# A hybrid decoder layer on one core: the last three planned blocks are ordered with lagging engines and loads, and the output stage's last operand is made behind its second product

## The chip, the cores and the metric

The kernel runs on one core of one Trainium2 chip. The core has five engines with a queue each: TensorE (PE, matrix products; its weight loads are listed as PEld), VectorE (DVE), ScalarE (ACT), GpSimd (POOL) and SyncE (SP), which here issues the DMAs. Every engine works through its own queue in order, and an instruction waits on semaphores for what other engines or DMAs must have finished. The metric is the device time of one execution, in microseconds (us), taken as the median of several runs. Before the change it is 1078.72 us.

## What is computed

One layer over 1024 rows of width 1024, all in 32-bit floats. The input is normalised and modulated, projected, and goes through four mixers A to D; each mixer's output, gated, is projected back to the full width by its `w_br`, weighted by a sigmoid gate from `h @ w_merge`, and summed. One last projection, a gate per column and a final norm follow:

```python
mod = (jax.nn.silu(c) @ w_ada + b_ada)[:, None, :]
shift, scale, gate = jnp.split(mod, 3, axis=-1)
h = rms_norm(x, norm_g) * (1.0 + scale) + shift
...                     # h @ w_in, split into 16 parts, four mixers
merged = None
for i, (y, z) in enumerate(branches):
    yi = y.reshape(B, S, BRANCH_W) * jax.nn.silu(z)
    term = jax.nn.sigmoid(h @ w_merge[i]) * (yi @ w_br[i])
    merged = term if merged is None else merged + term
x = x + gate * (merged @ w_out)
return rms_norm(x, final_g)
```

Four products of 1024 x 1024 x 1024 with `w_merge` and one with `w_out` are the bulk of the second half of the kernel, which is the half that the change touches.

## The kernel before, in words

**Products.** A 32-bit operand is split into a rounded high part and a low part: ScalarE copies the source into the high tile (`whi<-wst`), and VectorE or GpSimd subtracts to get the low tile (`wlo<-wst,whi`). A product is then three passes of matmuls, high x high, high x low and low x high. The 2 x 2 block products are done in seven products in place of eight: sums and differences of blocks are formed first (`s<-wst`, `wst<-wst,wst`), and sums of results after. One `product` (12 matmuls of 128 x 512: four depths of three passes) fills one bank of TensorE's output memory; the banks are called `s`, `t`, `d`, `y` with a number, and VectorE adds a finished bank to a tile `mt`, which frees it. `op(n)` makes the split of the stationary operand of product n, with the sums that it needs.

**Stages.** The first block holds everything up to the mixers and ends near 583 us. The *pair stage* (`noted(tc, 8000.0)` at L1824, 582 to 938 us) takes 14 pairs of output tiles, seven products each, 98 in all. `op(7 * q + 6)` ends a pair's operands and calls for the merge weights of a later pair: two loads of 512 KB, into the tiles `wst` 0 and 1, which are the only two, so that a load waits for the split that reads the last content. Small loads `pst` (128 KB, `w_br`) and `ga` (`w_ada`) go out between them on the same queue. The modulation's gate is summed up here too, on VectorE (`gate_sum`), and finished column by column with a 128 x 1 matmul (`gate_end`); behind the eighth the vector `gatec` is written to DRAM as `gd`, 1024 elements of four bytes.

The *merge tail* (`noted(tc)` at L1884, 938 to 985 us) does the two output tiles left over without the seven-product form, loads `w_out` (`wr`, four loads of 1 MB) and prepares its sums and splits (`tt`, `hh`, `hl`, `yh`, `yl`). The *output stage* (`noted(tc)` at L1957, 985 to 1078 us) makes four groups of seven products with `w_out`, numbers 102 to 129. Its last moving operand is `wt4`, split from the parts that the tail left in `wst`; then `gd` and `final_g` are loaded over them, spread on all partitions (`gateb`, `fgb`), and VectorE multiplies the results by `gateb`, adds `x`, and writes the normed rows out.

**What sets the order.** Each block is first only noted: `note` records every instruction with its label, its predecessors and an estimated length. `schedule` then plays the block through with these estimates: an engine takes, of its ready instructions, the one with the lowest priority number, and the resulting starts set the order of emission. A priority is the rank of noting plus a number from a table, `SHIFT_PE` for TensorE and `SHIFT` for the others, looked up by the label, such as `('op', 97)`, `('out', 106)` (a product and what follows it), or `('tile', 3)`; a label that isn't in the table gets 0 or 10000. `late` is the time to which VectorE, ScalarE and GpSimd are taken to be busy with the block before; TensorE and SyncE are taken as free at 0. Every instruction is emitted by one line of `issue`, L380 before, L426 in the changed kernel, so that the profile tells groups apart by their tiles alone.

Of the kernel before, what the change touches and what calls it, by code (L numbers as in the profile page):

```python
# [88 lines left out]
def chunks(w):  # L89
# [28 lines left out]
    ('item', 3): 3000, ('item', 4): 1000, ('item', 7): 100, ('item', 9): 7000, ('out', 102): -10000,  # L118
    ('out', 103): 330, ('out', 106): -10030, ('out', 107): 10000, ('out', 109): 0, ('out', 110): 0,
    ('out', 111): 3000, ('out', 112): 9987, ('out', 113): 30, ('out', 114): 10000,  # L120
    ('out', 115): 10000, ('out', 117): -10, ('out', 119): -10890, ('out', 120): -30,
    ('out', 121): 3000, ('out', 122): -10000, ('out', 123): 10027, ('out', 124): 294,
    ('out', 126): -10800, ('out', 128): 10000, ('out', 129): 10000, ('out', 94): 0,
    ('out', 95): -10, ('out', 96): 10303, ('out', 97): -13, ('sum', 1): 9900, ('sum', 2): -10000,
    ('tile', 0): -9700, ('tile', 1): 3936, ('tile', 10): -10030, ('tile', 11): -9727,
    ('tile', 13): 10000, ('tile', 14): 0, ('tile', 15): -370, ('tile', 16): -10000,
    ('tile', 17): 9700, ('tile', 18): -10400, ('tile', 19): 0, ('tile', 21): -100,
    ('tile', 25): 10600, ('tile', 26): 9970, ('tile', 27): -400, ('tile', 28): 0,
# [26 lines left out]
    ('item', 28): -10010, ('item', 29): 20000, ('item', 3): 3000, ('item', 30): 10100,  # L155
# [4 lines left out]
    ('mod', 6): -10, ('mod', 7): 20000, ('mod', 8): 0, ('op', 100): -1000, ('op', 101): 100,  # L160
# [5 lines left out]
    ('op', 98): -9980, ('op', 99): 10, ('out', 102): 10100, ('out', 103): -1000, ('out', 104): 30,  # L166
    ('out', 107): -9863, ('out', 108): 10, ('out', 109): 0, ('out', 110): 10000, ('out', 111): 0,
    ('out', 112): -300, ('out', 113): 0, ('out', 114): -3, ('out', 115): 10000, ('out', 116): 2700,
    ('out', 118): 10, ('out', 119): 30, ('out', 120): 10970, ('out', 121): -10030,
    ('out', 122): 3000, ('out', 123): 0, ('out', 124): 30, ('out', 126): -10, ('out', 129): 9990,  # L170
    ('out', 93): 0, ('out', 94): -10100, ('out', 95): 30, ('out', 96): -103, ('out', 97): 8990,
    ('split', 0): 0, ('split', 1): 30, ('split', 2): 9700, ('split', 3): 1000, ('split', 4): -10300,
    ('split', 5): 0, ('split', 6): -100, ('sum', 0): 0, ('sum', 1): 0, ('sums', 0): 9700,
    ('sums', 1): 10097, ('sums', 2): 2057, ('tile', 15): 19630, ('tile', 23): -1300,
# [260 lines left out]
def hybrid_kernel(ctx: ExitStack, tc: tile.TileContext, x, c, w_ada, b_ada, norm_g, w_in, cmp_pos,  # L435
                  cmp_w1, cmp_w2, sink, w_merge, w_br, w_out, final_g, kb, km, kd, ks, kw, out):
    nc = tc.nc
    md = Program()
# [564 lines left out]
    with ac:  # L1003
# [607 lines left out]
    with ExitStack() as mc:  # L1611
# [449 lines left out]
```

## Time and profile before

| what | before |
|---|---|
| median of 3 runs | 1078.72 us (1078.55 to 1079.52) |
| profiled execution | 1079.71 us, its span 1077.9 us |
| TensorE busy | 1040.4 us, 97% of the span |
| VectorE, ScalarE, GpSimd busy | 796.5, 584.4 and 435.5 us |
| mean granted clock of TensorE | 0.988 |
| moved by DMA | 105.47 MB |

The span runs from the first to the last instruction; the profiled execution's time has 1.8 us more around it. Busy TensorE time counts matmuls, which are pipelined: a matmul of 128 x 512 lasts 0.39 us in the records, but the next starts about 0.23 us behind it when the clock is at its full 2.4 GHz, and 0.43 us behind it at 1.2 GHz, the lower of the two levels. The granted clock of a stretch is 1.00 when it was at the upper level throughout.

### The profile page before, as it was taken

The numbers are of one execution on the slowest core, as the hardware profiler recorded it, in microseconds if no ns is written. First come the engines' busy times: TensorE is split into PE (matmuls) and PEld (weight loads), VectorE is DVE, ScalarE is ACT, GpSimd is POOL, SyncE is SP. The second block draws the span as 40 slices with busy tenths as digits, with TensorE's granted clock in tenths as the row PEclk, the third lists the DMA queues.
The fourth block names the chain that finished last, engine by engine and source line by source line (L and its number), as shares of the span: only waits on it lengthen the run. The fifth ranks groups of instructions, "written<-read, shape, count | busy, mean of one in ns | idle before, by whom it ended". The sixth has DMA issues, their size and how long they took to land.

```text
span 1077.9 us, 16022 instructions
## 1 busy us (share of the span) xinstructions
PE 1040.4 (97%) x5391; PEld 873.4 (81%) x5391; DVE 796.5 (74%) x1797; ACT 584.4 (54%) x1281; POOL 435.5 (40%) x483
## 2 busy tenths in 40 slices
PE   5999999999999999999999999999999999998996
PEld 4778888889878898888888788888888888876885
DVE  5559976986558877999875346777785565489897
ACT  5699964994348866767874232333333233346343
POOL 4623214213525466655464122255454555430002
PEclk8999999999999999999999999999999999999998
DMA  9763311102321113314313913322322232262232
GB/s 338 259 201 80 83 25 48 33 21 59 54 79 40 30 40 101 107 62 134 103 55 124 350 53 88 98 69 69 88 88 58 54 90 73 73 230 74 77 107 95
DMA packets 117606, 105.47 MB, mean 98 GB/s; under 512 B 15260, under 2 KB 96212, under 8 KB 116756
## 3 DMA queue, kind: packets, MB, share of 16 engines
q1 hardware_dynamic: 116048, 99.95, 30.3%
q0 software_dynamic: 1408, 4.48, 1.3%
q8 instruction: 42, 0.69, 0.3%
q14 instruction: 40, 0.33, 0.1%
q10 hardware_dynamic: 68, 0.02, 0.0%
HBM read 81.88 MB, written 17.83 MB: 93 GB/s over the span
## 4 chain that ended last, share of the span: by engine, by line
PE 70%; DVE 11%; ACT 6%; issue 5%; DMA 5%; POOL 2%; SPq 1%; POOLq 0%; ACTq 0%; DVEq 0%
PE d L380 25%; PE s L380 22%; PE t L380 14%; PE y L380 8%; DVE SP L380 4%; ACT t L380 2%; DVE lo L380 1%; DMA wst<-in_w_merge_dram 1%; DVE t L380 1%; ACT SP L380 1%; ACT whi L380 1%; DVE FA L380 1%; POOL RA L380 1%; DMA RA<-RA 1%; ACT hi L380 1%
## 5 line engine op out<-in xcount | busy, mean ns | idle before, releaser
L380 POOL TENSOR_TENSOR wlo<-wst,whi 128x512 fp32r<-128x512 f32 (+1 forms) x108 | 143.3, 1337 | 214.4 <-ACT whi L380 208.8
L380 PE MATMUL d<-hh,whi 128*128 128x512 f32 x440 | 180.5, 410 | 2.5 <-ACT hh L380 1.8
L380 ACT ACTIVATE whi<-wst 128x512 fp32r<-128x512 f32 (+2 forms) x121 | 89.0, 739 | 164.7 <-PE s L380 47.3
L380 PE MATMUL d<-hh,wlo 128*128 128x512 f32 x440 | 173.4, 394 | 0.0
L380 PE MATMUL d<-hl,whi 128*128 128x512 f32 x440 | 173.0, 394 | 0.0
L380 PEld LDWEIGHTS d<-hh,wlo 128*128 128x128 f32 x440 | 83.4, 190 | 18.7
L380 PEld LDWEIGHTS d<-hh,whi 128*128 128x128 f32 x440 | 83.6, 190 | 15.3 <-ACT hh L380 2.0
L380 DVE TENSOR_TENSOR lo<-t,hi 128x512 fp32r<-128x512 f32 (+2 forms) x132 | 79.8, 624 | 18.2 <-ACT hi L380 17.4
L380 PEld LDWEIGHTS d<-hl,whi 128*128 128x128 f32 x440 | 83.5, 190 | 11.6 <-DVE hl L380 0.4
L380 ACT ACTIVATE hi<-t 128x512 fp32r<-128x512 f32 (+3 forms) x148 | 73.8, 525 | 31.4 <-PE t L380 26.9
L380 POOL TENSOR_TENSOR acc<-acc,mt 128x512 f32<-128x512 f32 x44 | 68.0, 1547 | 44.3 <-DVE mt L380 43.7
L380 PE MATMUL s<-hh,whi 128*128 128x512 f32 x200 | 80.4, 402 | 3.9 <-ACT whi L380 3.9
L380 PE MATMUL s<-hh,wlo 128*128 128x512 f32 x200 | 79.7, 398 | 0.9 <-DVE wlo L380 0.9
L380 PE MATMUL s<-hl,whi 128*128 128x512 f32 x200 | 78.5, 394 | 0.0
L380 PE MATMUL t<-kbt,SP 128*128 128x128 f32 (+1 forms) x470 | 68.3, 274 | 6.8 <-DMA kbt<-in_kb_dram 6.4
L380 POOL TENSOR_SCALAR SP<-SP,den,gates 128x640 f32<-128x640 f32 (+7 forms) x64 | 52.9, 835 | 52.9 <-DVE den L380 20.7
L380 ACT ACTIVATE SP<-SP,mx 128x257 f32<-128x257 f32 (+9 forms) x96 | 62.3, 651 | 11.9 <-DVE mx L380 10.7
L380 DVE TENSOR_TENSOR mt<-s,mt 128x512 f32<-128x512 f32 x61 | 41.2, 686 | 36.4 <-PE s L380 36.1
L380 PEld LDWEIGHTS t<-kbt,SP 128*128 128x128 f32 (+1 forms) x470 | 54.7, 141 | 14.2 <-DMA kbt<-in_kb_dram 6.4
L380 PE MATMUL s<-tt,whi 128*128 128x512 f32 x192 | 59.1, 389 | 0.0
L380 ACT ACTIVATE mt<-mt 128x512 f32<-128x512 f32 x56 | 35.1, 629 | 35.4 <-DVE mt L380 35.2
L380 ACT ACTIVATE t<-t 128x512 f32<-128x512 f32 (+5 forms) x97 | 50.1, 522 | 1.1
(343 smaller groups left out, 2717.7 us busy)
## 6 DMA issues: line engine op xcount, KB each, us to landing
wst<-in_w_merge_dram SPq DMA_DIRECT2D x32, 512.0 KB, 4.8
wst<-in_w_in_dram SPq DMA_DIRECT2D x26, 512.0 KB, 3.9
td<-FA SPq DMA_DIRECT2D x32, 256.0 KB, 2.4
tt<-td SPq DMA_DIRECT2D x6, 1024.0 KB, 10.2
FA<-in_x_dram SPq DMA_DIRECT2D x8, 512.0 KB, 5.5
pst<-in_w_br_dram SPq DMA_DIRECT2D x32, 128.0 KB, 2.2
ga<-in_w_ada_dram SPq DMA_DIRECT2D x16, 256.0 KB, 3.1
wr<-in_w_out_dram SPq DMA_DIRECT2D x4, 1024.0 KB, 9.1
```

The lines of the kernel that those rows point to most:

```text
L380: fn(*args, **kw)
```

## The change

Both tables get new entries for the pair stage, the tail and the output stage (some 80 and some 170 labels that had none); those of the first block stay, and so does the first block's order. `schedule` takes TensorE's clock as full from the start and the first DMA as busy until `late + 1100` wherever `late` is set; the tail gets `late` 2000 and the output stage 6000, where both had 0. In `pair`, `op(7 * q + 6)` is noted ahead of the fourth product and of the `yield`; for the last pair, whose rest is noted in the tail, this moves that call into the pair stage. In the output stage the `wt4` parts and the loads of `gateb` and `fgb` are noted behind the second product instead of at the start.

```diff
@@ SHIFT_PE, SHIFT
-    ('tile', 4): 20000, ('tile', 5): 10300, ('tile', 6): -10000, ('tile', 7): 1000,
+    ('tile', 8): 0, ('tile', 9): -2700,
...
@@ schedule
-        dma = warm = 0.0
+        dma, warm = (self.late + 1100.0, 3400.0) if self.late else (0.0, 0.0)
@@ pair
             add(u3, o, u2)
+            op(7 * q + 6)
             yield
             o = product(7 * q + 3, MOVING[3])
-            op(7 * q + 6)
             add(g11, o, t1)
@@ merge tail
-        with md.noted(tc):
+        with md.noted(tc, 2000.0):
             for t, kh, n in ((r11, 0, 0), (r12, 0, 1), (r22, 1, 1), (r21, 1, 0)):
@@ output stage
-        with md.noted(tc):
-            md.label = "wt4", 0
-            for k in range(4):
-                parts(wt4, k, t4f[k], ve)
-            sy.dma_start(gateb, gd.partition_broadcast(P))
-            sy.dma_start(fgb, final_g.partition_broadcast(P))
+        with md.noted(tc, 6000.0):
             x_load(0)
...
                 o = product(b + 1, MOVING[1])
                 op(b + 4)
+                if q == 0:
+                    md.label = "wt4", 0
+                    for k in range(4):
+                        parts(wt4, k, t4f[k], ve)
+                    sy.dma_start(gateb, gd.partition_broadcast(P))
+                    sy.dma_start(fgb, final_g.partition_broadcast(P))
                 add(u2, o, t1)
```

The number of instructions is the same on every engine; what follows is their order at three places.

SyncE's queue in the pair stage, around the write of `gd` (`wst_125` and `wst_126` are the two tiles for merge weights). Before:

```order
L380 DMA wst_125<-in_w_merge_dram 128x8x128
L380 DMA wst_126<-in_w_merge_dram 128x8x128
L380 DMA gd<-gatec 128x8x1
L380 DMA pst_5774<-in_w_br_dram 128x2x128
L380 DMA pst_5776<-in_w_br_dram 128x2x128
L380 DMA wst_125<-in_w_merge_dram 128x8x128
L380 DMA wst_126<-in_w_merge_dram 128x8x128
```

And in the changed kernel:

```order
L426 DMA wst_125<-in_w_merge_dram 128x8x128
L426 DMA gd<-gatec 128x8x1
L426 DMA wst_126<-in_w_merge_dram 128x8x128
L426 DMA pst_5774<-in_w_br_dram 128x2x128
L426 DMA pst_5776<-in_w_br_dram 128x2x128
L426 DMA pst_5774<-in_w_br_dram 128x2x128
L426 DMA wst_125<-in_w_merge_dram 128x8x128
L426 DMA wst_126<-in_w_merge_dram 128x8x128
```

Before, `gd` is followed by two `pst` loads and then by the two merge loads of a later pair; now the first of these two stands ahead of `gd` and the second directly behind it.

VectorE at the same place, from the gate sum on (`s_5801<-wst_126` reads the merge load just spoken of; `d_132` and `d_133` are two of TensorE's banks). Before:

```order
L380 TENSOR_TENSOR gatec<-d_133,gatec 128x1
L380 SCALAR_TENSOR_TENSOR mt_5806<-mt_5806,y_137 128x512
L380 TENSOR_TENSOR mt_5803<-s_136,mt_5802 128x512
L380 TENSOR_TENSOR wlo_142<-wst_125,whi_141 128x512
L380 TENSOR_TENSOR mt_5807<-t_127,mt_5803 128x512
L380 TENSOR_TENSOR mt_5805<-t_140,mt_5802 128x512
L380 TENSOR_TENSOR mt_5802<-d_132,mt_5803 128x512
L380 TENSOR_TENSOR mt_5804<-d_132,mt_5807 128x512
L380 TENSOR_TENSOR s_5801<-wst_126 128x512
L380 SCALAR_TENSOR_TENSOR mt_5805<-mt_5805,d_133 128x512
L380 TENSOR_TENSOR wst_126<-wst_125,wst_126 128x512
```

And now:

```order
L426 TENSOR_TENSOR gatec<-d_133,gatec 128x1
L426 SCALAR_TENSOR_TENSOR mt_5806<-mt_5806,y_137 128x512
L426 TENSOR_TENSOR mt_5803<-s_136,mt_5802 128x512
L426 TENSOR_TENSOR mt_5807<-t_127,mt_5803 128x512
L426 TENSOR_TENSOR s_5801<-wst_126 128x512
L426 TENSOR_TENSOR mt_5804<-d_132,mt_5807 128x512
L426 TENSOR_TENSOR wst_126<-wst_125,wst_126 128x512
L426 TENSOR_TENSOR mt_5807<-s_135,mt_5807 128x512
L426 TENSOR_TENSOR wlo_142<-wst_125,whi_141 128x512
L426 TENSOR_TENSOR mt_5805<-t_140,mt_5802 128x512
L426 TENSOR_TENSOR mt_5802<-d_132,mt_5803 128x512
L426 SCALAR_TENSOR_TENSOR mt_5805<-mt_5805,d_133 128x512
```

The sum that reads the merge load now stands four instructions behind the gate sum and ahead of the sums that free the banks `t_140` and `d_132`, where before it stood behind them; the product with `d_133` is the eighth instruction from it, where it was the second.

VectorE at the start of the merge tail, now (the first rows of the tail's block; `s_136` and `t_127` are banks, `wlo_139` the low part of the tail's first operand):

```order
L426 TENSOR_TENSOR mt_5805<-s_136,mt_5802 128x512
L426 TENSOR_TENSOR wlo_139<-wst_125,whi_138 128x512
L426 TENSOR_TENSOR mt_5802<-t_127,mt_5803 128x512
L426 TENSOR_TENSOR mt_5804<-t_127,mt_5807 128x512
L426 TENSOR_TENSOR wlo_139<-wst_125,whi_138 128x512
L426 SCALAR_TENSOR_TENSOR mt_5805<-mt_5805,d_133 128x512
L426 TENSOR_TENSOR tt_5798<-wr_8152,tt_5798 128x512 x4
```

Before, the same stretch was:

```order
L380 TENSOR_TENSOR tt_5798<-wr_8148,tt_5798 128x512 x3
L380 TENSOR_TENSOR mt_5805<-s_136,mt_5802 128x512
L380 TENSOR_TENSOR wlo_139<-wst_125,whi_138 128x512 x2
L380 TENSOR_TENSOR mt_5802<-t_127,mt_5803 128x512
L380 TENSOR_TENSOR mt_5804<-t_127,mt_5807 128x512
L380 SCALAR_TENSOR_TENSOR mt_5805<-mt_5805,d_133 128x512
```

The three `tt` parts no longer stand ahead, and the product with `d_133` is the sixth instruction.

VectorE at the start of the output stage (`s_5801` is the source of product 106's operand, `wst_125` becomes `gateb`; `wt_8475` is `wt4`). Before:

```order
L380 TENSOR_TENSOR acc<-acc 128x4x128
L380 TENSOR_TENSOR wt_8475<-wst_125,wt_8475 128x512 x2
L380 TENSOR_TENSOR wt_8475<-wst_126,wt_8475 128x512 x2
L380 TENSOR_TENSOR wlo_139<-s_5801,whi_138 128x512
L380 TENSOR_TENSOR s_5801<-acc 128x512
L380 TENSOR_TENSOR mt_5803<-d_132,mt_5802 128x512
L380 TENSOR_TENSOR wlo_139<-acc,whi_138 128x512
L380 TENSOR_TENSOR mt_5806<-s_134,mt_5803 128x512
```

And now:

```order
L426 TENSOR_TENSOR acc<-acc 128x4x128
L426 TENSOR_TENSOR mt_5803<-d_132,mt_5802 128x512
L426 TENSOR_TENSOR wlo_139<-s_5801,whi_138 128x512
L426 TENSOR_TENSOR wlo_139<-acc,whi_138 128x512
L426 TENSOR_TENSOR mt_5806<-s_134,mt_5803 128x512
L426 TENSOR_TENSOR s_5801<-acc 128x512
L426 TENSOR_TENSOR wlo_142<-acc,whi_141 128x512
L426 TENSOR_TENSOR wt_8475<-wst_125,wt_8475 128x512 x2
L426 TENSOR_TENSOR mt_5804<-s_136,mt_5806 128x512
L426 TENSOR_TENSOR wt_8475<-wst_126,wt_8475 128x512 x2
```

ScalarE there, before:

```order
L380 ACTIVATE hh<-wr_8148 128x512
L380 ACTIVATE whi_141<-acc 128x512
L380 ACTIVATE wt_8475<-wst_125 128x512 x2
L380 ACTIVATE wt_8475<-wst_126 128x512 x2
L380 ACTIVATE whi_138<-s_5801 128x512
L380 ACTIVATE mt_5802<-t_140 128x512
```

And now:

```order
L426 ACTIVATE mt_5802<-t_140 128x512
L426 ACTIVATE whi_138<-s_5801 128x512
L426 ACTIVATE whi_138<-acc 128x512
L426 ACTIVATE wt_8475<-wst_125 128x512 x2
L426 ACTIVATE whi_141<-acc 128x512
L426 ACTIVATE wt_8475<-wst_126 128x512 x2
L426 ACTIVATE whi_141<-acc 128x512
```

On both engines the parts of `wt4` went behind the split of `s_5801`; on VectorE six instructions came in between the sum in `acc` and the first `wt`.

## Rows read from the trace of the kernel before

**Rows 1.** Busy time of the engines on the page
```profile
PE 1040.4 (97%) x5391; PEld 873.4 (81%) x5391; DVE 796.5 (74%) x1797; ACT 584.4 (54%) x1281; POOL 435.5 (40%) x483
```
**Rows 2.** Waits of TensorE from 600 to 1080 us: total, times, longest
```profile
PE s L380 <- ACT whi L380: 3.9, 2, 3.0
PE s L380 <- DVE wlo L380: 0.9, 2, 0.7
PE d L380 <- ACT whi L380: 0.2, 1, 0.2
```
**Rows 3.** Table by stage: length, busy time of each engine, clock, DMA share, GB/s
```profile
700.00:760.00 60.00, 60.00 (x269) 49.77 (x268) 45.03 (x69) 20.39 (x36) 32.18 (x26) 1.00 0.22 64
938.00:950.00 12.00, 10.46 (x43) 7.97 (x42) 5.84 (x10) 4.71 (x9) 1.29 (x1) 0.94 0.94 292
980.00:1000.00 20.00, 16.76 (x61) 12.84 (x60) 15.35 (x26) 10.64 (x20) 0.00 (x0) 0.83 0.42 156
1000.00:1040.00 40.00, 40.00 (x178) 33.12 (x177) 37.65 (x62) 15.55 (x32) 1.68 (x3) 1.00 0.23 79
```
**Rows 4.** TensorE in time, start of the merge tail: start, length, waits in brackets
```profile
946.60 0.50 PE L380 MATMUL s<-hh,whi 128*128 128x512 f32 x1 [0.88 <-ACT whi L380]
948.00 0.50 PE L380 MATMUL s<-hh,wlo 128*128 128x512 f32 x1 [0.67 <-DVE wlo L380]
948.57 0.60 PE L380 MATMUL d<-hl,whi 128*128 128x512 f32 x1
951.96 0.42 PE L380 MATMUL d<-yh,phi 128*128 128x512 f32 x1
```
**Rows 5.** Chain of waits, 935 to 1000 us: start, length, what
```profile
938.28 5.80 DMA wr<-in_w_out_dram
971.22 6.12 PE s L380 x27
```
**Rows 6.** TensorE in time, start of the output stage
```profile
993.24 0.80 PE L380 MATMUL s<-hh,whi 128*128 128x512 f32 x1 [2.99 <-ACT whi L380]
994.72 0.80 PE L380 MATMUL s<-hh,wlo 128*128 128x512 f32 x1 [0.25 <-DVE wlo L380]
999.58 0.50 PE L380 MATMUL d<-hl,whi 128*128 128x512 f32 x1
```
**Rows 7.** ScalarE in time, both places
```profile
945.92 1.15 ACT L380 ACTIVATE whi<-wst 128x512 fp32r<-128x512 f32 x2
990.48 2.19 ACT L380 ACTIVATE wt<-wst 128x512 fp32r<-128x512 f32 x4 [2.75 <-DVE hl L380]
```
**Rows 8.** VectorE in time, start of the output stage
```profile
990.96 0.69 DVE L380 TENSOR_TENSOR acc<-acc 128x512 f32<-128x512 f32 x1
991.56 2.50 DVE L380 TENSOR_TENSOR wt<-wst,wt 128x512 fp32r<-128x512 f32 x4
```
**Rows 9.** SyncE's queue in time, output stage
```profile
992.88 0.33 SPq L380 DMA_DIRECT2D wst<-gd  x1
```
**Rows 10.** The tensor gd: landing times of its write and its read
```profile
DMA to landing us min/median/max: 6.8/8.9/11.0
```
**Rows 11.** DMA issues on the page: count, KB, median us to landing
```profile
wst<-in_w_merge_dram SPq DMA_DIRECT2D x32, 512.0 KB, 4.8
```
**Rows 12.** SyncE's queue in time, pair stage
```profile
831.48 0.37 SPq L380 DMA_DIRECT2D gd<-gatec  x1
832.05 6.46 SPq L380 DMA_DIRECT2D pst<-in_w_br_dram  x2
```
**Rows 13.** TensorE in time, the last gate matmul
```profile
830.40 0.28 PE L380 MATMUL d<-ga,ga 128*128 128x1 f32 x2
```
**Rows 14.** DMA issues from 826 to 850 us
```profile
wst<-in_w_merge_dram SPq DMA_DIRECT2D x2, 512.0 KB, 9.4
pst<-in_w_br_dram SPq DMA_DIRECT2D x2, 128.0 KB, 12.0
```
**Rows 15.** VectorE in time, behind the write of gd
```profile
850.17 0.89 DVE L380 TENSOR_TENSOR s<-wst 128x512 f32<-128x512 f32 x1 [3.08 <-DMA wst<-in_w_merge_dram]
```

More of the change, by code (lines that the diff above doesn't have):

```diff
@@ L117 @@
     ('item', 22): 9990, ('item', 24): 10000, ('item', 27): 10100, ('item', 29): 10000,
[L118 to L128, printed above, removed]
@@ L129 @@
-    ('tile', 29): 11000, ('tile', 3): -10000, ('tile', 30): 10030, ('tile', 31): 63,
-    ('tile', 4): 20000, ('tile', 5): 10300, ('tile', 6): -10000, ('tile', 7): 1000,
-    ('tile', 9): -10000,
+    ('item', 3): 3000, ('item', 4): 1000, ('item', 7): 100, ('item', 9): 7000, ('out', 0): -2990,
+    ('out', 1): 0, ('out', 102): -30, ('out', 103): 0, ('out', 104): 0, ('out', 105): 0,
+    ('out', 106): -10000, ('out', 107): 10, ('out', 108): 30, ('out', 109): -10, ('out', 11): 10000,
+    ('out', 110): -11190, ('out', 111): -10303, ('out', 112): 0, ('out', 113): -9000,
@@ new lines @@
+    ('out', 114): 300, ('out', 117): 0, ('out', 118): -10010, ('out', 119): -10000,
+    ('out', 12): 10000, ('out', 120): 0, ('out', 121): -10010, ('out', 122): 0, ('out', 123): 10000,
+    ('out', 124): -100, ('out', 126): 10, ('out', 129): 10010, ('out', 13): 0, ('out', 14): 10000,
+    ('out', 15): 0, ('out', 16): 0, ('out', 18): 0, ('out', 19): -300, ('out', 2): -10000,
+    ('out', 21): -10000, ('out', 22): 9970, ('out', 24): -10000, ('out', 25): 9970, ('out', 27): 0,
+    ('out', 28): 10, ('out', 29): -1000, ('out', 3): -103, ('out', 32): 10013, ('out', 33): 9990,
@@ new lines @@
+    ('out', 35): -270, ('out', 36): 10000, ('out', 38): -30, ('out', 39): 0, ('out', 4): -1000,
+    ('out', 40): 19000, ('out', 41): -200, ('out', 42): 0, ('out', 43): -9990, ('out', 44): -10000,
+    ('out', 45): 0, ('out', 46): -10403, ('out', 48): 0, ('out', 49): -20, ('out', 5): -100,
+    ('out', 50): -10000, ('out', 51): 1000, ('out', 53): -10060, ('out', 54): 10000,
+    ('out', 55): 93, ('out', 56): -667, ('out', 57): 270, ('out', 58): -10000, ('out', 60): 100,
+    ('out', 61): 100, ('out', 62): 9033, ('out', 63): 0, ('out', 64): 0, ('out', 65): 690,
@@ new lines @@
+    ('out', 67): 9930, ('out', 69): 0, ('out', 7): -7000, ('out', 71): -10000, ('out', 72): -110,
+    ('out', 74): 0, ('out', 75): 9970, ('out', 77): 0, ('out', 79): -200, ('out', 8): -10000,
+    ('out', 80): -7000, ('out', 81): 10000, ('out', 82): 0, ('out', 84): 6000, ('out', 86): -10003,
+    ('out', 87): 9990, ('out', 88): -10000, ('out', 9): -990, ('out', 90): -13000,
+    ('out', 91): 9990, ('out', 93): -11000, ('out', 94): -10000, ('out', 95): -10000,
+    ('out', 97): -10000, ('sum', 1): 9900, ('sum', 2): -10000, ('tile', 0): 100, ('tile', 1): 3,
@@ new lines @@
+    ('tile', 10): 9970, ('tile', 11): -10010, ('tile', 12): 0, ('tile', 14): -10100,
+    ('tile', 15): 100, ('tile', 16): 0, ('tile', 17): -70, ('tile', 19): -10000, ('tile', 2): 0,
+    ('tile', 20): -9900, ('tile', 21): -10000, ('tile', 22): -9000, ('tile', 24): 10000,
+    ('tile', 26): 400, ('tile', 27): 303, ('tile', 28): -300, ('tile', 29): -3003, ('tile', 3): -30,
+    ('tile', 30): 0, ('tile', 4): -3000, ('tile', 5): -10100, ('tile', 6): 9997, ('tile', 7): 0,
+    ('tile', 8): 0, ('tile', 9): -2700,
@@ L154 @@
     ('item', 23): 8680, ('item', 24): 30, ('item', 25): 18900, ('item', 26): 0, ('item', 27): 8670,
-    ('item', 28): -10010, ('item', 29): 20000, ('item', 3): 3000, ('item', 30): 10100,
+    ('item', 28): -10010, ('item', 29): 20000, ('item', 3): 3000, ('item', 30): -13000,
     ('item', 4): 990, ('item', 5): 12027, ('item', 8): -9990, ('item', 9): -10030, ('mod', 0): 0,
@@ L159 @@
     ('mod', 21): 0, ('mod', 23): 0, ('mod', 3): 0, ('mod', 4): 9990, ('mod', 5): -3000,
-    ('mod', 6): -10, ('mod', 7): 20000, ('mod', 8): 0, ('op', 100): -1000, ('op', 101): 100,
[5 rows of a table removed]
[L166 to L174, printed above, removed]
[5 rows of a table removed]
+    ('mod', 6): -10, ('mod', 7): 20000, ('mod', 8): 0, ('op', 0): -100, ('op', 1): 10030,
[22 rows of a table added]
@@ new lines @@
+    ('out', 10): -60, ('out', 102): 0, ('out', 103): -1000, ('out', 104): 1020, ('out', 105): -10,
+    ('out', 107): 20000, ('out', 108): 0, ('out', 11): 0, ('out', 110): -970, ('out', 112): -9210,
+    ('out', 113): -300, ('out', 115): 10303, ('out', 117): 10000, ('out', 119): 0, ('out', 12): -30,
+    ('out', 120): 43, ('out', 121): -1010, ('out', 122): -2700, ('out', 123): 0, ('out', 124): 9900,
+    ('out', 126): -10100, ('out', 129): 10213, ('out', 13): 10000, ('out', 15): 300, ('out', 16): 0,
@@ new lines @@
+    ('out', 17): -1013, ('out', 18): 20000, ('out', 19): 10030, ('out', 2): 0, ('out', 20): 10000,
+    ('out', 21): 30, ('out', 23): -10, ('out', 24): 0, ('out', 25): 970, ('out', 27): -10010,
+    ('out', 28): 20000, ('out', 29): 0, ('out', 3): 100, ('out', 30): 9970, ('out', 31): -1200,
+    ('out', 33): 10000, ('out', 34): 10000, ('out', 35): 10300, ('out', 36): -10000,
+    ('out', 37): 9900, ('out', 38): -8697, ('out', 39): -9600, ('out', 4): 0, ('out', 40): 6260,
+    ('out', 41): 0, ('out', 42): -1100, ('out', 43): 20000, ('out', 44): 0, ('out', 45): 600,
@@ new lines @@
+    ('out', 46): -10, ('out', 48): -30, ('out', 49): 10000, ('out', 5): 2700, ('out', 50): 10000,
+    ('out', 51): -11000, ('out', 52): 19870, ('out', 53): 0, ('out', 54): -2900, ('out', 56): -7697,
+    ('out', 57): -10300, ('out', 58): 10000, ('out', 59): -10037, ('out', 6): 0, ('out', 60): 0,
+    ('out', 64): 10000, ('out', 66): -9990, ('out', 67): 30, ('out', 68): 0, ('out', 69): 0,
+    ('out', 7): 3000, ('out', 70): -1000, ('out', 71): -10000, ('out', 72): 100, ('out', 73): 9900,
+    ('out', 74): 0, ('out', 75): 10000, ('out', 76): 0, ('out', 77): 6700, ('out', 78): -30,
@@ new lines @@
+    ('out', 79): -3000, ('out', 8): 0, ('out', 80): 0, ('out', 82): -10010, ('out', 84): -9000,
+    ('out', 85): -1010, ('out', 86): 300, ('out', 87): -9940, ('out', 89): 10000, ('out', 9): 8970,
+    ('out', 91): -9970, ('out', 92): 0, ('out', 94): -10, ('out', 95): -1000, ('out', 96): 0,
+    ('out', 97): -10, ('split', 0): 0, ('split', 1): 30, ('split', 2): 9700, ('split', 3): 1000,
+    ('split', 4): -10300, ('split', 5): 0, ('split', 6): -100, ('sum', 0): 0, ('sum', 1): 0,
+    ('sums', 0): 9700, ('sums', 1): 10097, ('sums', 2): 2057, ('tile', 31): 0, ('w', 0): -100,
[5 rows of a table added]
```

37 rows, old and new, of the table SHIFT are left out of this document.

## The prediction, made before the changed kernel ran

> **What bounds the kernel now.** I read the page's first part, then the waits of TensorE, then its rows in time with a table by stage, and last the queue of SyncE. TensorE is busy for 1040.4 us, 97% of the span [rows 1]: it is the bound, and whatever the change does counts only as TensorE time without a matmul or with a matmul at half clock. From 600 us on its waits are 3.9 us for `whi`, 0.9 us for `wlo` and 0.2 us, and nothing else [rows 2]. The table by stage says where [rows 3]: in the pair stage (60 of 60 us busy, granted clock 1.00) there is none to win; in 938 to 950 and in 980 to 1000 TensorE is busy for 10.46 of 12 and 16.76 of 20 us, at a mean clock of 0.94 and 0.83.
>
> The two places in time: at the start of the merge tail a matmul starts at 946.60 after 0.88 us for `whi` and one at 948.00 after 0.67 us for `wlo`, and then eight steps from 948.57 to 951.96 take 0.42 us each [rows 4]. A step at the full 2.4 GHz is 6.12 us / 27 = 0.227 us [rows 5]; these run at the lower of the two levels, 1.2 GHz. At the start of the output stage the wait is 2.99 us, and the 13 steps from 993.24 to 999.58 take 6.34 us with a wait of 0.25 us among them [rows 6]. So the change can take away: waits 0.88 + 0.67 + 2.99 + 0.25 = 4.8 us; eight steps at 0.42 - 0.23, 1.6 us; thirteen steps, 6.34 - 0.25 - 13 x 0.227, 3.1 us; about 0.15 us of restart at each of four waits (946.60 to 948.00 is 0.5 us longer than its two steps and its wait), 0.6 us. Together 10.1 us. The tables of the first block are as they were, and TensorE's order in it too: I give it nothing.
>
> **Output stage.** Before, ScalarE makes four `wt` parts (2.19 us) from 990.48 on, and only then the split `whi<-s` for which TensorE waits until 993.24 [rows 6, 7]; VectorE has its four `wt` parts (2.50 us, 0.60 us each) ahead of the `wlo` [rows 8]. In the changed order of ScalarE this `whi<-s` stands ahead of the `wt` rows, and TensorE has products 102, 103 and 104 ahead of 106: 36 matmuls or 8.2 us, where before it ran dry 21 matmuls behind its entry. What stays on the path is VectorE's last work of the tail, its sum at 990.96 [rows 8]: that, `whi` and `wlo` at 0.6 us each, and one sum between, make 993.4, where TensorE, having entered at 993.24 - 2.99 - 0.15 - 21 x 0.227 = 985.3, comes to the product at 993.5. I take a wait of 0.3 us (0 to 1.5, as VectorE's row is one or two instructions longer there) and no half clock.
>
> The load of the gate vector can go out only when VectorE is through with the first two `wt`, whose buffer it fills. It went out at 992.88 [rows 9], behind the four loads of `x`, with 6.8 us to landing [rows 10]. Those two `wt` now stand six instructions later, so it goes out at 996.5, with the loads of `x` mostly in; a merge load of the same size has 4.8 us [rows 11], so it lands at 1001.3. VectorE first needs it three instructions behind the end of TensorE's fifth product, 985.3 + 60 x 0.227 + 0.3 + 1.8 = 1001.0. I take 0.2 us (0 to 2.3, when it flies for 6.8 us again); VectorE is busy for 37.65 of 40 us in this stage [rows 3] and can catch up little. Gain: 2.99 + 0.25 + 3.1 + 0.3 - 0.5 = 6.1 us.
>
> The Trainium skill ("DMA: Bandwidth & Descriptors", section "Rules for kernel authors") speaks against this edit: a DMA is to be issued early and waited for late, so that its fixed cost lies under compute. The trace agrees in so far as the 6.8 us before lay under other work whole; by the rule the 3.6 us of later issue would be paid, and the sum would be some 2 us worse.
>
> **Merge tail.** `op(7q + 6)` ahead of the `yield` brings its two loads and the split into the pair stage's block. One of the loads still stands behind the first `wr` in SyncE's queue, and that `wr` takes 5.80 us from 938.28 [rows 5]; so `whi<-wst` can't start much before its 945.92 of before [rows 7]. What changes is who waits. Before, it was the tile product at 946.60. Now TensorE has the branch matmuls and another product first, and comes to the tile only 16 groups of three (10.9 us) behind its entry at 938.1, at 949.0. But at 14 groups (9.5 us, 947.6) it writes the bank `d_133` again, which VectorE frees as its sixth instruction: split on ScalarE to 946.5, then `wlo`, two sums, `wlo`, and the product with `d_133`, five at 0.60 us, to 949.6. A wait of 2.0 us (1 to 2.5) takes the place of 0.88 + 0.67. The half clock followed two short waits there before [rows 4]; behind one longer wait I take 0.8 us (0 to 1.7) and 0.15 us of restart. Gain: 0.88 + 0.67 + 1.6 + 0.3 - 2.0 - 0.8 - 0.15 = 0.5 us (-1 to 2.3).
>
> **Pair stage.** Its engines and loads are now taken to lag, so that loads and splits stand nearer to their use, in an order made from the new tables. As nothing waits there before, this can only cost. Most such moves are hidden by the room that the loads have. One isn't, the write of the gate vector, `gd`. Before, it went out at 831.48 [rows 12], 1.08 us behind the gate matmul at 830.40 [rows 13], and took 11.0 us to landing [rows 10]; the small `pst` load 0.57 us behind it took 12.0 us and the merge loads 9.4 [rows 12, 14], against 4.8 us for a merge load over the whole run [rows 11]. So a load issued right behind `gd` lands only after it. TensorE felt nothing: the merge loads came 7.5 us and more behind `gd`, and VectorE, which waited 3.08 us for the second (`s<-wst` at 850.17) [rows 15], had its sums for TensorE's banks ahead of it.
>
> In the changed queue that second merge load stands directly behind `gd`. With t the start of the gate matmul: `gd` goes out at t + 1.1 and lands at t + 12.1. The load lands at least 1.6 us later, which the first `pst`, a quarter of its size, needed (12.0 + 0.57 - 11.0), and at most 3.1 us: in the 7.7 us from `gd`'s landing at 842.5 to 850.2 four loads of 1.25 MB together came in, of which it is 0.5 MB. That is t + 13.7 to t + 15.2; I take t + 14.5. VectorE meets `s<-wst` four instructions behind its gate sum and waits. From it to the multiplication with the bank `d_133` (`mt_5805<-mt_5805,d_133`) are eight instructions at 0.60 us, and 0.4 us more for the first [rows 8, 15]: 5.2 us, so the bank is free at t + 19.7. TensorE writes this bank again 20 groups of three behind the gate matmul: 60 x 0.227 + 0.2 = t + 13.8. It waits 5.9 us (5.1 to 6.6). Behind the wait of 2.99 us the clock cost 3.1 us [rows 6]; I take 2.9 us here (0 to 3.4). The place costs 8.8 us (5 to 10). For other places with less room I take 0.5 us (0 to 3).
>
> On this the Trainium skill has two sentences in "DMA: Bandwidth & Descriptors". By "Rules for kernel authors" a non-contiguous last dimension becomes one descriptor for each element, as the write of `gatec` through its `(k p)` view does; the 11.0 us for 4 KB agree. By "Queues, rings and completion order" each DMA engine takes its ring in order, but completion over a queue isn't in order; a load could slip past `gd` where it lies on other engines, and that is the first rival.
>
> **The sum.** Output stage -6.1 us, tail -0.5, pair stage +9.3: +2.7 us. The profiled execution took 1079.71 us (a span of 1077.9 and 1.8 us around it), 1.0 us over the median of 1078.72. On the profile this makes 1082.4, on the median 1081.4 us, my forecast.
>
> **Rivals.**
> 1. The pair stage stays without waits: the load behind `gd` isn't held, or VectorE has room that I don't see. For it: 60 of 60 us busy before [rows 3], and a wait of VectorE of 3.08 us that cost nothing. Against: the 12.0 us of the `pst` in the very same place in the queue. Then the gains remain, 6.6 us: 1072 us.
> 2. The pair stage loses in many places: loads of 4.8 us meet splits that stand directly behind them, VectorE (45 of 60 us busy, [rows 3]) falls back behind the `gd` wait and doesn't catch up, and each short wait like that of 946.60 to 948.00 brings a half-clock stretch worth 1.6 us. One or two more of these, 1.5 us of wait with 1.6 us of clock, come to 3 to 6 us on top: 1084.5 to 1087.5 us. Against: VectorE is the engine waited for nowhere in that stage before.
> 3. Half of the `gd` wait is absorbed, as the load lands at its early bound and the clock falls for a short stretch: 5 to 7 us lost against 6.6 won, 1077 to 1080 us, no change.
> 4. The output stage gains little, as VectorE's last work in the tail comes 3 us later than at 990.96: its wait of 2.99 us and the half clock stay, the gain falls from 6.1 to about 1 us, and the kernel takes 1086.5 us. It decides once that sum begins after 994.
>
> **Chances.** What a measurement of this kernel can tell from no change is 0.2%, 2.2 us: from 1076.6 to 1080.9. The forecast with its own range of 1079 to 1084 has 0.42, of which 0.08 lies under 1080.9. Rival 1 has 0.33, rival 3 0.14 (0.02 of it under 1076.6), rival 2 0.08, rival 4 0.03. Faster: 0.33 + 0.02 = 0.35; same: 0.08 + 0.12 = 0.20; slower: 0.34 + 0.08 + 0.03 = 0.45. The range for 8 in 10 goes from 1071 to 1086 us: it cuts the far end of rival 1 and the upper ones of rivals 2 and 4.
>
> **What would show it.** In the profile after: a wait of TensorE of 5 to 7 us on VectorE's `mt` some 14 us behind the last gate matmul, half clock behind it, and the merge load behind `gd` at over 12 us to landing. At the output stage no wait of 2.99 us for `whi<-s`, and full clock at its entry; in the tail a wait of about 2 us at `d_133` 9.5 us behind its entry in place of the two for the tile. Wrong: no wait of TensorE over 1 us in the pair stage, or the load behind `gd` landing in 5 us (rival 1).

## The result, and the profile after

The changed kernel takes 1086.41 us (median of 5 runs, 1083.06 to 1088.65), the kernel before 1078.55 us beside it: a ratio of 1.0074, 95% interval 1.0051 to 1.0097. Run once more beside other kernels it took 1087.98 us against 1078.19, 1.0092 (1.0078 to 1.0106). It is slower, as forecast, but by 8 to 10 us where 2.7 were forecast. The profiled execution, the slowest of the five, took 1088.65 us with a span of 1086.9.

The busy time of the engines in the profile after, against [rows 1]; the columns are the same:

```profile
PE 1040.7 (96%) x5391; PEld 872.9 (80%) x5391; DVE 791.3 (73%) x1797; ACT 586.2 (54%) x1281; POOL 435.8 (40%) x483
```

TensorE's waits from 580 us on, total, times, longest, against [rows 2]:

```profile
PE d L426 <- DVE mt L426: 11.3, 3, 5.8
PE s L426 <- DVE mt L426: 0.5, 1, 0.5
PE t L426 <- POOL wlo L426: 0.5, 1, 0.5
PE s L426 <- ACT whi L426: 0.5, 1, 0.5
```

The work is the same; the waits went from 5.0 to 12.8 us, and what ends them, the splits before, is now in 11.8 of the 12.8 us a sum of VectorE in `mt`. The table by stage, against [rows 3] (length, busy time of each engine, granted clock, DMA share, GB/s):

```profile
700.00:760.00 60.00, 58.06 (x256) 47.21 (x255) 44.29 (x67) 19.15 (x34) 28.85 (x23) 1.00 0.27 77
...
860.00:900.00 40.00, 37.23 (x156) 30.65 (x157) 23.64 (x31) 15.09 (x27) 22.28 (x17) 0.91 0.25 76
...
950.00:980.00 30.00, 25.95 (x105) 20.98 (x104) 19.89 (x30) 8.85 (x16) 6.82 (x6) 0.89 0.70 240
980.00:1000.00 20.00, 20.00 (x90) 16.57 (x89) 19.30 (x31) 12.69 (x21) 3.67 (x3) 1.00 0.00 1
1000.00:1040.00 40.00, 40.00 (x178) 33.10 (x178) 38.92 (x65) 18.20 (x38) 2.10 (x2) 1.00 0.37 131
```

TensorE now loses in the pair stage, which was full before, and in the tail; from 980 us on it is full at a clock of 1.00. The entry of the output stage, at 1000.95, has no wait at all.

Where the 9.0 us between the two spans (1077.9 and 1086.9) lie shows in the starts of the first matmuls of the blocks, read from the traces. All lengths in us, from a block's first matmul to the next block's (the pair stage from one `s<-hh,wlo` near 583.5 us, the same one in all kernels; the output stage to the start of its last matmul); the kernels e1 to e10 are told below:

| kernel | pair stage | tail | output stage | median | ratio to before (95%) |
|---|---|---|---|---|---|
| before | 354.6 | 47.2 | 82.9 | 1078.5 | |
| changed | 366.6 | 50.1 | 76.2 | 1086.41 | 1.0074 (1.0051 to 1.0097) |
| e1 output stage alone | 354.2 | 45.4 | 76.2 | 1072.17 | 0.9944 (0.9931 to 0.9958) |
| e2 tail alone | 354.7 | 43.5 | 83.5 | 1076.89 | 0.9988 (0.9979 to 0.9998) |
| e3 pair stage alone | 367.6 | 48.2 | 82.7 | 1093.16 | 1.0139 (1.0125 to 1.0153) |
| e4 tail and output stage | 354.3 | 43.5 | 76.2 | 1069.59 | 0.9923 (0.9911 to 0.9936) |
| e5 load ahead of `gd` | 360.4 | 48.3 | 76.2 | 1082.19 | 1.0039 (1.0025 to 1.0052) |
| e6 `gd` in rows | 357.4 | 48.4 | 76.2 | 1078.84 | 0.9996 (0.9985 to 1.0007) |
| e7 `w_out` behind the load | 366.0 | 45.1 | 76.2 | 1083.69 | 1.0049 (1.0035 to 1.0063) |
| e8 e5 and e7 | 361.4 | 44.5 | 76.2 | 1078.62 | 1.0006 (0.9995 to 1.0017) |
| e9 `gd` priced in the planner | 359.8 | 48.4 | 76.2 | 1079.32 | 1.0013 (1.0003 to 1.0022) |
| e10 changed, again | 365.4 | 49.5 | 76.2 | 1087.98 | 1.0092 (1.0078 to 1.0106) |

Of the 9.0 us the pair stage has +12.1, the tail +2.8, the output stage -6.7, and the first block +0.7. The first block has the same order in both traces on every engine (one of its labels, `('item', 30)`, did get another number); it takes from 582.7 to 586.2 us over these twelve profiles, so that single profiles aren't to be compared by their spans to better than about 2 us. The stages agree better: the pair stage in its old order takes 354.2 to 354.7 us in four profiles.

**The write of `gd`.** The three rows of SyncE's queue, with start and length, against [rows 12]:

```profile
842.36 0.37 SPq L426 DMA_DIRECT2D wst<-in_w_merge_dram  x1
843.98 0.37 SPq L426 DMA_DIRECT2D gd<-gatec  x1
844.44 0.53 SPq L426 DMA_DIRECT2D wst<-in_w_merge_dram  x1
```

VectorE there (idle time and its releaser in brackets), against [rows 15]:

```profile
843.80 0.15 DVE L426 TENSOR_TENSOR gatec<-d,gatec 128x1 f32<-128x1 f32 x1
...
857.46 0.69 DVE L426 TENSOR_TENSOR s<-wst 128x512 f32<-128x512 f32 x1 [9.29 <-DMA wst<-in_w_merge_dram]
...
862.03 0.69 DVE L426 SCALAR_TENSOR_TENSOR mt<-mt,d 128x512 f32<-128x512 f32 x1
```

And TensorE, whose gate matmul is the t of the prediction, against [rows 13]:

```profile
843.00 0.28 PE L426 MATMUL d<-ga,ga 128*128 128x1 f32 x2
...
862.77 0.80 PE L426 MATMUL d<-yh,phi 128*128 128x512 f32 x1 [5.77 <-DVE mt L426]
...
867.09 0.39 PE L426 MATMUL y<-yl,phi 128*128 128x512 f32 x1
```

The load lands by t + 14.5, as taken (VectorE starts on it at 857.46, 13.0 us behind its issue); VectorE, which waited 3.08 us at no cost before, waits 9.29; `d_133` is free at t + 19.7, and TensorE waits 5.77 us where 5.9 were forecast. The ten steps from 862.77 to 867.09 take 4.32 us, 2.05 more than at the full clock.

**Smaller waits, at 711, 757, 806 and 810 us.** VectorE and GpSimd ahead of the first:

```profile
704.48 0.69 DVE L426 TENSOR_TENSOR s<-wst 128x512 f32<-128x512 f32 x1 [2.10 <-DMA wst<-in_w_merge_dram]
...
706.28 1.78 DVE L426 TENSOR_TENSOR wlo<-wst,whi 128x512 fp32r<-128x512 f32 x1
707.99 1.77 DVE L426 TENSOR_TENSOR wst<-s,wst 128x512 f32<-128x512 f32 x1
```

```profile
705.97 1.56 POOL L426 TENSOR_TENSOR wlo<-s,whi 128x512 fp32r<-128x512 f32 x1 [5.99 <-ACT whi L426]
707.48 1.73 POOL L426 TENSOR_TENSOR wlo<-wst,whi 128x512 fp32r<-128x512 f32 x1
```

TensorE waits 1.46 us at 711.01 for the sum behind these. By the rows two causes add up, which no run takes apart: a merge load that came 2.10 us late for VectorE, and two of VectorE's instructions that took 1.8 us instead of 0.68 while GpSimd was at work. The Trainium skill has the second ("SBUF — State Buffer", section "SBUF: two separate sides"): a VectorE instruction with two inputs in that memory and one of GpSimd that reads it exclude each other for their whole length. The rows agree, with 1.1 us for each. Before the change VectorE had such instructions too, without a TensorE wait behind them:

```profile
827.92 1.66 DVE L380 TENSOR_TENSOR wst<-wst 128x512 f32<-128x512 f32 x1
```

The waits at 806 and 810 come and go with who starts first. In the changed kernel GpSimd starts a split 0.05 us ahead of a sum of VectorE, and the sum takes 1.80 us:

```profile
803.91 1.30 POOL L426 TENSOR_TENSOR wlo<-wst,whi 128x512 fp32r<-128x512 f32 x1 [3.82 <-ACT whi L426]
803.96 1.80 DVE L426 TENSOR_TENSOR wst<-wst,wst 128x512 f32<-128x512 f32 x1
```

In e10, a second profile of the same kernel, VectorE starts the same sum 0.15 us ahead of GpSimd, and it is GpSimd that takes longer:

```profile
803.62 0.68 DVE L426 TENSOR_TENSOR wst<-wst,wst 128x512 f32<-128x512 f32 x1
803.77 1.70 POOL L426 TENSOR_TENSOR wlo<-wst,whi 128x512 fp32r<-128x512 f32 x1 [3.76 <-ACT whi L426]
```

A second sum, three instructions on, goes the same way (1.78 us, and 0.68 in e10). In the changed kernel and in e3, e5, e8 and e9 both sums are slow and TensorE waits at both places; in e6, e7 and e10 neither is, and it waits at neither. The wait at 757, for a split of GpSimd, is in all eight profiles with the new order of the pair stage, as is the one at 711; its cause stays open.

**The tail.** ScalarE, VectorE and TensorE, against [rows 4, 7]; a fence for each:

```profile
960.80 0.63 ACT L426 ACTIVATE whi<-wst 128x512 fp32r<-128x512 f32 x1 [9.27 <-DMA wst<-in_w_merge_dram]
```

```profile
951.75 0.68 DVE L426 TENSOR_TENSOR wlo<-wst,whi 128x512 fp32r<-128x512 f32 x1
...
963.87 0.68 DVE L426 SCALAR_TENSOR_TENSOR mt<-mt,d 128x512 f32<-128x512 f32 x1
```

```profile
950.87 0.39 PE L426 MATMUL s<-hh,whi 128*128 128x512 f32 x1
...
964.60 0.79 PE L426 MATMUL d<-yh,phi 128*128 128x512 f32 x1 [4.05 <-DVE mt L426]
...
969.42 0.39 PE L426 MATMUL s<-hh,wlo 128*128 128x512 f32 x1
```

The split starts 9.9 us behind TensorE's entry (950.87), where it was 7.8 before (938.09 to 945.92). SyncE's queue tells why, against [rows 5]:

```profile
951.92 0.47 SPq L426 DMA_DIRECT2D wr<-in_w_out_dram  x1
952.80 0.37 SPq L426 DMA_DIRECT2D wst<-in_w_merge_dram  x1
953.22 5.57 SPq L426 DMA_DIRECT2D wr<-in_w_out_dram  x3
```

The merge load goes out 1.9 us behind the entry instead of 1.0, since the split at 951.75 still read its buffer, and behind `wr`, which goes out 1.1 us behind the entry instead of 0.2. The load then takes 7.9 us, against 6.8 before. Of the wait of 4.05 us, 2.1 us are this lateness, about half of it the later issue and half the longer flight; the other 2.0 are what was forecast.

### The profile page after: what moved, and what is told of

Read it like the earlier page. It is cut to its first block, busy times and chain, and to the rows that moved or that the text cites. A ratio compares the mean times of both kernels' runs of the same rounds, so it can differ in the third digit from the quotient of the medians.

```text
span 1086.9 us, 15950 instructions
## 1 busy us (share of the span) xinstructions
PE 1040.7 (96%) x5391; PEld 872.9 (80%) x5391; DVE 791.3 (73%) x1797; ACT 586.2 (54%) x1281; POOL 435.8 (40%) x483
## 4 chain that ended last, share of the span: by engine, by line
PE 66%; DVE 14%; DMA 8%; ACT 6%; issue 3%; POOL 3%; POOLq 0%; SPq 0%; DVEq 0%; ACTq 0%
PE d L426 24%; PE s L426 20%; PE t L426 13%; PE y L426 8%; DVE SP L426 4%; DMA wst<-in_w_merge_dram 3%; DMA wst<-in_w_in_dram 2%; DVE lo L426 2%; DVE mt L426 2%; ACT t L426 1%; DVE t L426 1%; POOL wlo L426 1%; DMA FA<-in_x_dram 1%; ACT SP L426 1%; DVE FA L426 1%
## 5 line engine op out<-in xcount | busy, mean ns | idle before, releaser
L426 PEld LDWEIGHTS d<-hh,wlo 128*128 128x128 f32 x440 | 82.9, 188 | 18.5
L426 POOL TENSOR_TENSOR acc<-acc,mt 128x512 f32<-128x512 f32 x44 | 64.3, 1468 | 37.1 <-DVE mt L426 36.8
L426 DVE TENSOR_TENSOR wlo<-wst,whi 128x512 fp32r<-128x512 f32 x46 | 38.5, 839 | 26.9 <-ACT whi L426 26.3
L426 DVE TENSOR_TENSOR mt<-s,mt 128x512 f32<-128x512 f32 x61 | 41.3, 685 | 17.6 <-PE s L426 12.1
```

What stands on the lines that cost most here:

```text
L426: fn(*args, **kw)
```

## The experiments

**e1 to e4: which block does what.** A block gets the changed kernel's tables, lag and order, or those of before. In all of them `noted` has an argument that picks the tables and the planner's start values; e1 is

```diff
-        with md.noted(tc, 8000.0):
+        with md.noted(tc, 8000.0, False):
...
-        with md.noted(tc, 2000.0):
+        with md.noted(tc, 0.0, False):
```

with `op(7 * q + 6)` behind the product as before, and the other three are the other choices (e2 and e4 have the call ahead of the `yield` for the last pair alone).

> Theory: the three blocks act apart from each other, and the output stage took 6.7 us less from TensorE's entry to its last matmul. With that stage alone changed the kernel takes 1078.5 - 6.7, about 1072 us, and TensorE has no wait of 2.99 us at 990. Rival: the stage gained only because TensorE's waits ahead of it let VectorE and ScalarE catch up; without them the gain is 0 to 2 us, 1076.5 us or more.

> The tail alone changed, with the two loads of op(97) in the pair stage, which is otherwise as before. Theory: the tail lost 2.8 us because its first merge load was let go late by the pair stage's last split and stood behind the 1 MB load of w_out; here it stands ahead of that load, so the wait at d_133 is under 1 us and the tail gains 2 to 3.5 us: 1075 to 1076.5 us. Rival: the tail's new order by itself makes VectorE free d_133 late; a wait of 2 to 4 us stays and the time is 1079 to 1081 us.

> The pair stage alone changed, op(97) noted in the tail as before. Theory: the whole loss of 12.1 us lies in this stage, 8.9 of it at the write of gd and 3.2 at three smaller waits (711, 806, 810 us): 1088 to 1091 us. Rival: the gd wait alone is the pair stage's own, and the smaller ones come and go from run to run: 1086 to 1088 us.

> Tail and output stage changed, the pair stage as before with op(97) noted in it. Theory: the gains add up, 6.7 in the output stage and 2 to 3.5 in the tail: 1068 to 1070 us. Rival: the output stage's gain hangs on TensorE's earlier waits; then 1075 to 1078 us.

Measured: e1 -6.3 us, e2 -1.6, e3 +14.7, e4 -8.9 us. The output stage's gain stands by itself: the rival of e1 and e4 falls. In e2 and e4 the tail has no wait: with the pair stage in its old order the merge load that the tail's split needs goes out 1.1 us ahead of TensorE's entry and ahead of `wr`, and takes 4.3 to 4.4 us. In e2 the tail is 3.7 us shorter, but the old output stage, come to earlier, waits longer for the same split, as this row shows against the 2.99 us of [rows 6]:

```profile
992.14 0.80 PE L510 MATMUL s<-hh,whi 128*128 128x512 f32 x1 [4.07 <-ACT whi L510]
```

That costs 0.6 us in the output stage. The tail's order is worth 1.6 us by itself and 2.6 us on top of the output stage's (e4 against e1), and both together have no TensorE wait over 0.1 us left behind 580 us. The same stretches in e4:

```profile
938.00:950.00 12.00, 12.00 (x54) 9.95 (x53) 8.61 (x12) 5.83 (x11) 3.91 (x3) 1.00 0.95 323
950.00:980.00 30.00, 30.00 (x134) 24.84 (x133) 29.12 (x46) 15.32 (x25) 6.36 (x5) 1.00 0.31 116
980.00:1000.00 20.00, 20.00 (x90) 16.58 (x89) 19.62 (x34) 9.94 (x20) 0.00 (x0) 1.00 0.42 158
```

e3 is above what I expected: the pair stage is 13.0 us longer there, with a wait of 6.7 us at `gd` and the smaller ones at the same places (1.40 us at 711, 0.62, 0.40 and 0.51). The rival had the smaller ones come and go from run to run: those at 806 and 810 do, those at 711 and 757 don't.

**e5 and e6: what holds the load at `gd`.** e5 takes the planned order and swaps two DMAs; e6 changes only how `gd` is written:

```diff
+        sp = [i for i in order if self.ops[i].eng == "sp"]
+        ...                       # the write of gd goes behind the next DMA
-                    sy.dma_start(gd.rearrange("(k p) -> p k", p=P), gatec)
+                    sy.dma_start(gd.rearrange("(p k) -> p k", k=KC), gatec)
```

> The changed kernel with one swap in SyncE's queue: the merge load goes out ahead of the write of gd instead of behind it; every other row is the same. Theory: the load lands in 4 to 6 us, the wait of 5.8 us at d_133 and the half clock behind it go, 1086.4 - 8.9 = about 1077.5 us (1076 to 1079.5). Rival: VectorE is too far behind at this place for other reasons, and a wait of 2 to 4 us stays: 1081 to 1084 us.

> The changed kernel with the order of its queue kept, and gd written as 128 contiguous rows of 8 elements instead of 1024 single elements (the gate vector then stands in another order in DRAM, so the gate applied to the output is permuted). Theory: it is the elements that hold the queue; gd lands in 2 to 4 us, the load behind it in 4 to 6, and the time is that of the swap, about 1077.5 us. Rival: any small write to DRAM in this queue holds what is behind it, the load takes over 9 us and the time stays above 1082 us.

Measured: 1082.19 and 1078.84 us. I had expected the same of both, and e5 falls short, in the range of its rival. Its DMAs from 838 to 860 us (count, KB, median us to landing; of the two merge loads the changed kernel and e6 have only the first one's landing recorded, so that the figure is that one's):

```profile
wst<-in_w_merge_dram SPq DMA_DIRECT2D x2, 512.0 KB, 6.7
```

Those of e6:

```profile
wst<-in_w_merge_dram SPq DMA_DIRECT2D x2, 512.0 KB, 4.1
gd<-gatec SPq DMA_DIRECT2D x1, 4.0 KB, 2.6
```

And of the changed kernel from 835 to 860 us, against [rows 14]:

```profile
wst<-in_w_merge_dram SPq DMA_DIRECT2D x2, 512.0 KB, 8.3
gd<-gatec SPq DMA_DIRECT2D x1, 4.0 KB, 11.0
```

In e5 the load that goes out 0.5 us ahead of `gd` still takes 9.2 us (the two are 4.3 and 9.2), and a TensorE wait of 1.23 us stays; in e8, with the same swap, these are 10.5 and 2.52 us. So the single elements slow loads issued a little ahead of them too, and the place in the queue is the larger part of the loss but not all of it: with the swap the pair stage falls by 6.2 us. Written as 128 rows of 32 bytes the same 4 KB land in 2.6 us, VectorE starts on the load behind them 5.0 us behind its issue instead of 13.0, and the wait at this place is gone: the pair stage falls by 9.2 us. Of these, 8.0 are the wait of the changed kernel with its restart and half clock, and about 1.5 the waits at 806 and 810, which e6 happens not to have. The rival of e6 falls. e6 applies the gate in a permuted order, so it tells the time alone.

**e7 and e8: what makes the tail late.**

```diff
         with md.noted(tc, 2000.0):
+            md.pre = [lambda r=r: ve.memset(r[:, 0, 0:1], 0.0) for r in (r11, r12, r22, r21)]
```

> The changed kernel with the first merge load of the tail ahead of the four loads of w_out in SyncE's queue (four writes of one column by VectorE into the buffers of w_out make these loads wait; 0.3 us of VectorE). Theory: the load lands 4.5 us behind its issue instead of 7.9, the wait at d_133 falls from 4.05 us to 0.6, its half clock goes too: 4 to 5.5 us less, 1081 to 1082.5 us. Rival: the wait comes from the late release of the load's buffer by VectorE, not from the queue: 1085 us or more.

> The changed kernel with both of the above edits of the queue (the swap at gd, and w_out behind the merge load). Theory: 1086.4 - 8.9 - 4.5, 1072 to 1074 us, 3 to 4 us above the kernel with the pair stage as before (1069.6), which is the price of the pair stage's smaller waits. Rival: with these two waits gone others grow, 1077 us or more.

Measured: 1083.69 and 1078.62 us. In e7 the load takes 4.4 us, the wait is nearly gone, and the tail is 5.0 us shorter than in the changed kernel:

```profile
962.13 0.50 PE L430 MATMUL d<-yh,phi 128*128 128x512 f32 x1 [0.21 <-DVE mt L430]
```

The median gained 2.7 us against the first measurement and 4.3 against the second, where 4 to 5.5 were expected: 1083.69 us lies between the expectation and its rival. A wait of 0.80 us for a sum came up later in its tail. The position behind `wr` is the main cause and not the late release: the split comes 3.8 us earlier against TensorE's entry, 3.5 of them from the shorter flight and 0.3 from an earlier issue. e8 misses its mark as e5 did, by the wait of 2.52 us that stays at `gd`, and lies in its rival's range; its two gains add up (5.2 us in the pair stage, 5.6 in the tail).

**e9: the planner's price of `gd`.** The planner counts a DMA by its bytes:

```diff
+            if str(out.tensor.name).startswith("gd"):
+                n *= 880
             op.dur, op.size = (475.0, n) if eng == "sp" else (1000.0, n)
```

> The changed kernel, with one estimate of the planner mended: the write of gd counts as about 10 us of DMA instead of by its 4 KB. The order that comes out keeps the merge load behind gd (two small loads go ahead of it) but puts the sum that reads it eight instructions later on VectorE, behind both products with d_133. Theory: the wait at d_133 goes though the load lands as late as before (over 12 us behind its issue or near it), the pair stage is 8 to 9 us shorter, 1077.5 to 1079 us. Rival: the late load then stops ScalarE's split or a later product, and a TensorE wait of 3 us or more appears some 20 to 25 us behind the gate matmul: 1081 to 1084 us.

Measured: 1079.32 us, 7 to 9 us less than the changed kernel, 0.3 above the expected range and no faster than before. The merge load still lands late, 11.3 us behind its issue, but VectorE meets it 16.8 us behind the gate sum and doesn't wait:

```profile
842.71 0.15 DVE L428 TENSOR_TENSOR gatec<-d,gatec 128x1 f32<-128x1 f32 x1
...
856.42 0.69 DVE L428 SCALAR_TENSOR_TENSOR mt<-mt,d 128x512 f32<-128x512 f32 x1
...
859.54 0.98 DVE L428 TENSOR_TENSOR s<-wst 128x512 f32<-128x512 f32 x1
```

A wait of 1.25 us stays at `d_133`: the first merge load, 1.6 us ahead of `gd`, took 12.3 us, and ScalarE's split waited for it. So the loss at this place came from a cost that the planner didn't know; told of it, the same tables give an order without most of the loss there. The pair stage is still 5.2 us longer than before, by that wait and the four smaller ones.

**e10: once more.**

> The changed kernel once more, unchanged, beside the one above and with a second profile. Theory: the waits of 5.8 us at the write of gd and of 3 to 4 us in the tail are there again, the smaller ones within 1 us of before, and what differs between runs lies in the first block: 1083 to 1088 us. Rival: the waits in the pair stage come and go, and the time differs by them.

Measured: 1087.98 us, with waits of 6.35 us at `gd` and 2.78 us in the tail; with `wr` landing in 5.8 us instead of 7.0, the tail's wait is shorter. Of the smaller waits the ones at 711 (1.23 us) and 757 (0.58) are there and those at 806 and 810 are not. The expectation holds in the main, and so does a part of its rival: the pair stage is 1.2 us shorter than in the first profile.

## Why the prediction was right and wrong

- *Output stage*: right. Forecast a gain of 6.1 us, measured 6.7 in the profile and 6.3 alone (e1); no wait for `whi<-s`, none for the gate vector's load worth a row of TensorE.
- *The write of `gd`*: right. Forecast a wait of 5.9 us at t + 13.8, measured 5.77 there; with 2.05 us of clock and the restart 8.0 us, forecast 8.8. In e6, which takes its cause away, nothing of it is left.
- *"For other places with less room I take 0.5 us (0 to 3)"*: this step failed. Four waits, at 711, 757, 806 and 810 us, have 1.46 + 0.48 + 0.47 + 0.50 = 2.9 us and nearly 0.3 us of restart each: 4.0 us. In the second profile the first two alone are there, 2.4 us. I had looked only for loads. At 711 half of the lateness is VectorE slowed by GpSimd, and at 806 and 810 this decides whether there is a wait at all; the traces of before had it already (1.66 us for an instruction of 0.68, beside GpSimd, in the pair stage), and with less room between VectorE and TensorE it costs.
- *Tail, "A wait of 2.0 us (1 to 2.5)" and "0.8 us (0 to 1.7)" of clock*: this step was mis-sized. The mechanism, the bank and the instruction were right; the wait was 4.05 us (2.78 in the second profile) and the eleven steps behind it, 964.60 to 969.42, lost 2.3 us. I had let the merge load land 7.7 us behind TensorE's entry as before. It is let go by the pair stage's last split, and in the new pair stage that split comes later against TensorE: what I had forecast for the one stage I didn't carry into the next. e2 and e4, with the pair stage in its old order, have no wait there. The tail lost 2.8 us where I had a gain of 0.5.
- *The sum*: +2.7 us forecast, 9.0 in the profile. The tail came out 3.3 us worse and the pair stage 2.8 (3.5 worse at the smaller places, 0.8 better at `gd`), the output stage 0.6 better; the first block gave 0.7, for which nothing was forecast. 2.7 + 3.3 + 2.8 - 0.6 + 0.7 = 8.9.
- *The rivals*: 1086.41 us lies in the second's 1084.5 to 1087.5, in part by luck. It has the pair stage's short waits and VectorE as their cause; but the four lie ahead of the `gd` wait and not behind it, none has half clock behind it, and half of the excess comes from the tail, which this rival doesn't have. The first and the third fall by the wait at `gd`, the fourth by e1.
- *A slip without consequence*: "946.60 to 948.00 is 0.5 us longer than its two steps and its wait" is 1.40 - 2 x 0.227 - 0.67 = 0.28 us; for two waits this is the 0.15 us each that the sum takes.

## What to carry to other kernels

Where the bound engine has no wait in a stage, a new order of that stage can only lose; put the new order to the stages that wait, and try them apart: here two of three blocks are worth 8.9 us (e4, 0.8% faster than the kernel before), and the third loses 14.7 by itself. When an order is brought closer to need, price the transfers by their landing in the trace and not by their bytes, and walk the lateness of one stage on into the next, through the buffers that it releases.

## What the runs showed of the hardware that I had not expected

- A write of 1024 single elements (4 KB, 11.0 us) slows loads issued before it too, by very different amounts: a 512 KB load issued 1.6 us ahead took 5.7 to 12.3 us over five profiles (e3 the least, e9 the most), one issued 0.5 us ahead 9.2 (e5) and 10.5 us (e8), against 4.1 with the same bytes written in rows. A load issued 1.7 us ahead, with the second one between it and the write, took 4.3 and 4.5 us (e5, e8).
- Some 0.2 us of start time decide which of VectorE and GpSimd is held up: where GpSimd's split starts 0.05 us ahead, VectorE's sum takes 1.80 us; where the sum starts 0.15 us ahead, it takes 0.68, and the split 1.70 instead of 1.30.
- The clock behind a wait isn't told by the wait's length: behind 2.78 us (e10) and 2.99 us (e6) in the tail the steps took 0.43 us, at 1.2 GHz, while behind 3.35 us at the same place in e5 they ran on at the upper level. In e10, then in e5:

```profile
961.90 0.80 PE L426 MATMUL d<-yh,phi 128*128 128x512 f32 x1 [2.78 <-DVE mt L426]
962.49 0.63 PE L426 MATMUL d<-yl,phi 128*128 128x512 f32 x1
962.92 0.63 PE L426 MATMUL d<-yh,plo 128*128 128x512 f32 x1
```

```profile
959.46 0.50 PE L432 MATMUL d<-yh,phi 128*128 128x512 f32 x1 [3.35 <-DVE mt L432]
959.80 0.39 PE L432 MATMUL d<-yl,phi 128*128 128x512 f32 x1
960.03 0.39 PE L432 MATMUL d<-yh,plo 128*128 128x512 f32 x1
```
